# Ten more blocks turned by VectorE squares and memory, longer delays, branches mixer by mixer, in a decoder block on one core

## The chip, the cores and the metric

The kernel runs on one core of a Trainium2 chip. The metric is the device time of one execution in microseconds (us); of several executions the median is taken. Four engines share the work and run their own queues in order: TensorE (PE) multiplies and transposes, VectorE (DVE) and ScalarE (ACT) do the elementwise work, GpSimd (POOL) does a little of it and starts DMAs; SyncE (SP) only starts DMAs. An instruction waits at the head of its queue until its inputs are there and its output buffer is free, and all behind it on that engine wait with it.

## The reference

256 tokens of width 2048, float32, one layer. The functions of the parts are cut, and the lines of merged and of x are written shorter than they are.

```python
u = rms_norm(x, attn_norm[l])
proj = jnp.einsum('bsd,de->bse', u, w_in[l])
(fq, fk, fv, ff, cq, ckv, kpe, gqkv, gz, gb, ga, gate) = jnp.split(proj, split_idx, axis=-1)
o_fox = fox_mixer(fq, fk, fv, ff, fox_fgate_bias[l])
o_mla = mla_mixer(cq, ckv, kpe, mla_q_norm[l], mla_kv_norm[l], w_mla_uq[l], w_mla_ukv[l], cos, sin)
o_gdn = gdn_mixer(gqkv, gz, gb, ga, gdn_conv[l], gdn_a_log[l], gdn_dt_bias[l], gdn_out_norm[l])
gates = jax.nn.sigmoid(gate).reshape(B, S, N_BRANCHES, D_MODEL)
merged = sum(gates[:, :, b] * jnp.einsum('bsc,cd->bsd', o_b, w_branch[l, b]) for b, o_b in enumerate((o_fox, o_mla, o_gdn)))
x = x + jnp.einsum('bsd,de->bse', merged, w_out[l])
h = rms_norm(x, mlp_norm[l])
x = x + jnp.einsum('bsf,fd->bsd', jnp.square(jax.nn.relu(jnp.einsum('bsd,df->bsf', h, w_up[l]))), w_down[l])
```

The three mixers have 8 heads of 128 each. Fox is causal softmax attention with a learned decay, MLA is causal attention on compressed queries and keys, and the gated delta rule (gdn) takes its q, k and v from gqkv, 3072 channels, through a causal convolution over 4 tokens and silu:

```python
def causal_depthwise_conv(x, w):
    K, C = w.shape
    return lax.conv_general_dilated(x, w[:, None, :], window_strides=(1,), padding=[(K - 1, 0)],
                                    dimension_numbers=('NWC', 'WIO', 'NWC'), feature_group_count=C)
```

It then solves, in chunks of 64 tokens, a unit triangular system whose entries are damped by the decays between two tokens.

## The kernel before

**Gemms.** Every product with a large weight goes through `gemm`. A chunk of weights is two tiles of 128 rows by 512 columns: SP loads it as `raw`, ACT rounds it to `wh` (L258), DVE subtracts to get the rest `wl` (L259), and PE runs twelve matmuls of 512 columns: for two tiles of rows and two halves of the tokens, wh times the rounded activations (L265), wl times them (L266) and wh times their rest (L267). `raw` has four buffers, `wh` and `wl` three each. After each chunk `tick` counts down what `later` has put off, and runs what is due. After the last chunk of a block of 512 columns `evac` reads the two sums out of PSUM.

**Order.** A side generator is stepped once a chunk by `weave`, its instructions placed behind the casts of the last chunk (`behind`, through `anchor`). What a step issues, and after how many chunks, is thus written in the kernel; the order of each engine's queue is fixed when the program is built.

**Stages**, in microseconds of the profile's span: latents 0 to 84; MLA's projections to 125; Fox columns with MLA's attention beside them to 261; the output gate z with Fox's attention to 320; gqkv, six blocks, to 476; the branch gates, twelve blocks, to 768, with the delta rule (`gdn`) beside them until some 696; the three branch products (w_branch) to 902; w_out to 991; w_up and w_down to the end.

**Two ways to turn a block** (256 tokens by 512 channels into channels by tokens). `fox_evac` for the four blocks of q and k, and `gqkv_evac` for six, let PE do it: eight transposes of 128x128 into PSUM (L626 `ft`, L703 `cv`), from which ACT and DVE read: Fox's copies into `fqT` and `fkT` (L629 and below), or the convolution, an ACT scaling (L705) and three DVE steps (L707) for each of four groups of channels. `turned`, for the branch sums (`acc`), w_out's and w_up's results, uses no PE: DVE transposes squares of 32x32 (L1067) into the first half of a tile `zy`, POOL's queue writes that to memory (L1069, `turn<-zy`, 512 KB) and reads it back reordered with four DMAs (L1072, `zy<-turn`, 128 KB each), and consumers run TURN = 8 chunks later, counted by `tick`: for the branches `halves_of` makes `mH` (ACT, L1081) and `mL` (DVE, L1082).

**The delta rule's side work.** `gdn` spreads the decays: `gcT` (L772) goes to memory and comes back to all partitions as `E` (L777); after nine steps DVE subtracts (L783). Later a substitution of 31 steps runs on DVE (`fs` L859, `NT` L861), its result goes through memory (`td`, then `DT`, L875), and after eight steps DVE squares it into `D` (L884), which the 32-wide matmuls `pO` and `pD` (`blocks_of`, L892) read.

**Branches.** The loop goes over the four blocks n of columns, and within it over mixers 2, 0, 1; the sum of a block is complete, and turned, after its third mixer. `reload` brings Fox's and MLA's outputs back from memory (`of`, `om`). w_out's gemm takes the first 12 of 16 rows of tiles of two blocks before their last four (LATE).

**Start.** `x_prep` transposes x beside the first gemm and squares it on ACT for the norm (L195).

## Time and profile before

| | |
|---|---|
| median of 3 executions | 1689.87 us (1687.35 to 1692.42) |
| profiled execution | 1695.37 us |
| span of its trace | 1693.4 us |
| mean granted PE clock | 0.996 |
| POOL busy | 113.9 us, 7% |
| weight loads from memory (SP's queue) | 311.07 MB of 356.55 MB moved |

The profile is of one execution. L numbers are lines of the kernel before; busy shares are of the span, and an engine is idle where it waits. A row of PE's timeline has start, duration, line, operation and, in brackets, the idle time ahead of it with what ended it.

### The profile page before, as it was taken

Reading aid. Unit: us, or ns where it says so; the run is one execution under the profiler, and the core shown is the slowest. Engines: PE = TensorE matmul, PEld = TensorE weight load, DVE = VectorE, ACT = ScalarE, POOL = GpSimd, SP = SyncE. Lnnn points to the kernel's source line nnn. Section 1 sums busy time; section 2 is a strip of 40 time slices with the busy share of each in tenths; the row PEclk is TensorE's granted clock in tenths of the full one; section 3 lists DMA queues with packets and bytes.
Section 4 is the critical chain, followed back from the end, with each engine's and each line's share of the span. In section 5 each row is a group of like instructions: output and inputs, shape, how many; then the busy total and the mean of one; then the engine's idle time right before and its main releaser. Section 6 shows DMA issues by size and latency. Waiting matters only on the chain.

```text
span 1693.4 us, 21572 instructions
## 1 busy us (share of the span) xinstructions
PE 1672.5 (99%) x8035; PEld 1404.3 (83%) x8035; DVE 1029.7 (61%) x1423; ACT 811.2 (48%) x1035; POOL 113.9 (7%) x202
## 2 busy tenths in 40 slices
PE   9999999999999999999999999999999999999997
PEld 8998889978788788888878888888888888888886
DVE  5755447677668745746666666555655566546655
ACT  5555446555645433544444555433544344434543
POOL 0000000000010100001210101100110011001100
PEclk9999999999999999999999999999999999999999
DMA  7765554766667654877888887856886688668863
GB/s 237 203 173 181 158 170 133 228 187 186 172 175 212 201 162 138 279 217 240 272 271 275 261 229 246 242 191 196 240 257 203 194 243 237 199 193 235 239 207 138
DMA packets 191626, 356.55 MB, mean 211 GB/s; under 512 B 18040, under 2 KB 40224, under 8 KB 191008
## 3 DMA queue, kind: packets, MB, share of 16 engines
q1 hardware_dynamic: 177616, 311.07, 60.6%
q0 software_dynamic: 13296, 43.29, 8.6%
q8 instruction: 63, 1.03, 0.3%
q10 hardware_dynamic: 608, 0.79, 0.1%
q14 instruction: 43, 0.35, 0.1%
HBM read 331.50 MB, written 23.61 MB: 210 GB/s over the span
## 4 chain that ended last, share of the span: by engine, by line
PE 86%; DMA 5%; DVE 4%; issue 3%; POOL 1%; ACT 1%; SPq 0%; DVEq 0%; POOLq 0%; ACTq 0%
PE mm L266 25%; PE mm L267 25%; PE mm L265 25%; DVE wl L259 2%; DMA zy<-turn 1%; DMA raw<-in_w_out_dram 1%; DMA raw<-in_w_in_dram 1%; DVE fs L859 1%; ACT wh L258 1%; DVE NT L861 0%; PE bf L508 0%; PE bf L509 0%; PE bf L510 0%; PE mm L1202 0%; PE mm L1201 0%
## 5 line engine op out<-in xcount | busy, mean ns | idle before, releaser
L259 DVE TENSOR_TENSOR wl<-raw,wh 128x1024 fp32r<-128x1024 f32 (+3 forms) x552 | 663.0, 1203 | 523.1 <-ACT wh L258 520.6
L258 ACT CAST wh<-raw 128x1024 fp32r<-128x1024 f32 (+3 forms) x552 | 571.5, 1037 | 688.2 <-PE mm L267 635.1
L266 PE MATMUL mm<-wl,uH 128*128 128x512 f32 (+3 forms) x896 | 346.0, 386 | 2.8 <-DVE wl L259 2.8
L267 PE MATMUL mm<-wh,uL 128*128 128x512 f32 (+3 forms) x896 | 343.9, 384 | 0.0
L265 PE MATMUL mm<-wh,uH 128*128 128x512 f32 (+3 forms) x896 | 319.6, 386 | 1.3 <-ACT wh L258 1.3
L266 PE MATMUL mm<-wl,hH 128*128 128x512 f32 x512 | 199.2, 389 | 0.0
L267 PE MATMUL mm<-wh,hL 128*128 128x512 f32 x512 | 199.2, 389 | 0.0
L266 PEld LDWEIGHTS mm<-wl,uH 128*128 128x128 f32 x896 | 169.4, 189 | 35.6 <-DVE wl L259 5.8
L265 PEld LDWEIGHTS mm<-wh,uH 128*128 128x128 f32 x896 | 168.1, 189 | 31.6 <-ACT wh L258 1.7
L267 PEld LDWEIGHTS mm<-wh,uL 128*128 128x128 f32 x896 | 169.2, 189 | 29.5
L266 PE MATMUL mm<-wl,dH 128*128 128x512 f32 x480 | 186.9, 389 | 0.1
L267 PE MATMUL mm<-wh,dL 128*128 128x512 f32 x480 | 186.8, 389 | 0.0
L265 PE MATMUL mm<-wh,hH 128*128 128x512 f32 x512 | 178.4, 389 | 0.0
L265 PE MATMUL mm<-wh,dH 128*128 128x512 f32 x480 | 167.2, 389 | 0.0
L266 PEld LDWEIGHTS mm<-wl,hH 128*128 128x128 f32 x512 | 96.1, 188 | 20.0
L267 PEld LDWEIGHTS mm<-wh,hL 128*128 128x128 f32 x512 | 96.1, 188 | 20.0
L265 PEld LDWEIGHTS mm<-wh,hH 128*128 128x128 f32 x512 | 96.1, 188 | 19.9
L266 PEld LDWEIGHTS mm<-wl,dH 128*128 128x128 f32 x480 | 90.1, 188 | 19.3 <-DVE wl L259 0.5
L267 PEld LDWEIGHTS mm<-wh,dL 128*128 128x128 f32 x480 | 90.1, 188 | 18.6
L265 PEld LDWEIGHTS mm<-wh,dH 128*128 128x128 f32 x480 | 90.0, 188 | 18.6
L1072 POOL DMA_DIRECT2D zy<-turn x96 | 52.4, 553 | 101.5 <-ACT wh L258 32.8
L1069 POOL DMA_DIRECT2D turn<-zy x24 | 13.3, 556 | 646.1 <-DVE zy L1067 646.1
(425 smaller groups left out, 1776.5 us busy)
## 6 DMA issues: line engine op xcount, KB each, us to landing
raw<-in_w_in_dram SPq DMA_DIRECT2D x192, 512.0 KB, 3.9
raw<-in_w_up_dram SPq DMA_DIRECT2D x128, 512.0 KB, 4.3
raw<-in_w_down_dram SPq DMA_DIRECT2D x128, 512.0 KB, 4.6
raw<-in_w_branch_dram SPq DMA_DIRECT2D x48, 512.0 KB, 5.1
raw<-in_w_out_dram SPq DMA_DIRECT2D x32, 512.0 KB, 4.9
turn<-zy POOLq DMA_DIRECT2D x24, 512.0 KB, 3.3
zy<-turn POOLq DMA_DIRECT2D x96, 128.0 KB, 5.6
gd<-ge POOLq DMA_DIRECT2D x24, 256.0 KB, 4.8
```

The costliest lines, as they stand in the source:

```text
L258: h = A.copy(out=wh[:, :, :n], in_=raw[:, :, :n])
L259: l = V.tensor_tensor(out=wl[:, :, :n], in0=raw[:, :, :n], in1=wh[:, :, :n].bitcast(F32), op=ALU.subtract)
L265: PE.matmul(ps[t][:, :n], lhsT=lhsH(k, t), rhs=wh[:, kk, :n], start=(k == 0), stop=False)
L266: PE.matmul(ps[t][:, :n], lhsT=lhsH(k, t), rhs=wl[:, kk, :n], start=False, stop=False)
L267: PE.matmul(ps[t][:, :n], lhsT=lhsL(k, t), rhs=wh[:, kk, :n], start=False, stop=last)
L859: V.tensor_tensor(out=tmp[:, :, 0:i + 1], in0=T[:, :, 0:i + 1], in1=Nb[:, 0:i + 1, i].unsqueeze(1).broadcast_to([P, 16, i + 1]), op=ALU.mult)
L1069: nc.gpsimd.dma_start(out=d, in_=z)
L1072: nc.gpsimd.dma_start(out=y[32 * j:32 * j + 32].rearrange("a (g x) -> a g x", g=4), in_=dv[j])
```

## The change

`turned` stands further up and serves ten more blocks: the four of Fox's queries and keys (TURN, now 10 chunks of delay) and the six of gqkv (13 chunks). `fox_heads` (an ACT copy for each half of the tokens) and `by_channel` (two copies into `ch`), then `conv` in two parts, read from SBUF a turned block. The 80 PE transposes of those blocks are gone. The branches wait 9 chunks, w_out's blocks 8, w_up's 10. E is subtracted after 14 steps, D after 12, the substitution has more steps towards its end, and what needs the convolution waits for it (`convolved`). The branch loop has the mixers outside (0, 1, 2) and the columns inside, with all four sums in one long tile; the reloads start 80 steps into the gates beside the delta rule. w_out takes 8 rows of tiles ahead where it took 12. The squares of x are put behind the last casts of the first gemm.

```diff
-TURN = 8
-LATE = 12
+TURN = 10
...
         for t in range(2):
-            for q in range(4):
-                j = t2("junk")
-                A.activation(out=j, in_=xs[t][:, q * 512:(q + 1) * 512], func=AF.Square, accum_out=ssx[:, t, q:q + 1])
+            with behind():
+                for q in range(4):
+                    j = t2("junk")
+                    A.activation(out=j, in_=xs[t][:, q * 512:(q + 1) * 512], func=AF.Square, accum_out=ssx[:, t, q:q + 1])
...
-        e = me("fe")
+        e = fe[t] = me("fe")
         scaled_evac(e, ps, t)
-        pt = psx("ft").rearrange("p (a t) -> p a t", a=4)
-        for a in range(4):
-            PE.transpose(pt[:, a, :], e[:, a * P:(a + 1) * P], ident)
+        if t == 1:
+            turned([fe[0], fe[1]], *[lambda y, t=t: fox_heads(bi, y, t) for t in range(2)])
+
+    def fox_heads(bi, y, t):
+
         h0 = (bi % 2) * 4
-        if bi < 2:
-            A.activation(out=fqT[:, h0:h0 + 4, t * P:(t + 1) * P], in_=pt, func=AF.Copy, scale=-(HD ** -0.5))
-        else:
-            ev_copy(fkT[:, h0:h0 + 4, t * P:(t + 1) * P], pt)
+        d = (fqT if bi < 2 else fkT)[:, h0:h0 + 4, t * P:(t + 1) * P].rearrange("p k (g b) -> p k g b", b=32)
+        yt = y.rearrange("p (g t k b) -> p t k g b", g=4, t=2, k=4)[:, t]
+        A.activation(out=d, in_=yt, func=AF.Copy, scale=-(HD ** -0.5) if bi < 2 else 1.0)
...
+        turned([gx[0], gx[1]], lambda y: by_channel(y, bi), lambda y: conv(y, bi, 0), lambda y: conv(y, bi, 1), delay=13)
+
+    chans, convolved = {}, set()
+
+    def by_channel(y, bi):
+
+        u = chans[bi] = big("ch")[:, 0:1024].rearrange("p (k t) -> p k t", k=4)
+        yv = y.rearrange("p (g t k b) -> p t k g b", g=4, t=2, k=4)
+        for t in range(2):
+            ev_copy(u[:, :, t * P:(t + 1) * P].rearrange("p k (g b) -> p k g b", b=32), yv[:, t])
+
+    def conv(_, bi, a):
+        u = chans[bi]
+        y = t2("y").rearrange("p (a b) -> p a b", a=2)
+        for b in range(2):
+            c = 2 * a + b
+            ct = bi * 4 + c
+            A.activation(out=y[:, b, :], in_=u[:, c, :], func=AF.Copy, scale=cw[:, 72 + ct:73 + ct])
...
-        for _ in wait(9):
+        for _ in wait(14):
             yield
...
+            while not {(g, 1), (g + 2, 1)} <= convolved:
+                yield
...
             if i % 2 or i > 12:
                 yield
+            if i > 20:
+                yield
...
-        for _ in wait(8):
+        for _ in wait(12):
             yield
...
-    weave(gates(0, 12), chain(delta, *again))
-    run(delta)
+    mixers = both(delta, chain(idle(80), *again))
+    weave(gates(0, 12), mixers)
+    run(again[0])
...
-    for n in range(4):
-        acc = [t2("acc") for _ in range(2)]
-        for i, b in enumerate((2, 0, 1)):
+    acc = [big("acc") for _ in range(2)]
+    for b in range(3):
+        if b == 1:
+            run(again[1])
+        if b == 2:
+            run(mixers)
+        for n in range(4):
...
-    weave(gemm(by_tile(mH), by_tile(mL), w_out[0], 0, 16, [(n * 512, 512) for n in range(4)], out_evac, True), load_x2())
+    weave(gemm(by_tile(mH), by_tile(mL), w_out[0], 0, 16, [(n * 512, 512) for n in range(4)], out_evac, 8), load_x2())
```

Three places in the engines' queues. First DVE where the decays go out and come back as E, in gqkv's stage (`gcT` to memory, `E` from it, `y<-cv` the convolution, `wl` the weights' rest, one to a chunk; `zy<-gq` squares of a turned block). Before:

```order
L772 COPY gcT_3222<-pr_686_3220 16x128
L707 SCALAR_TENSOR_TENSOR y_706_3323<-cv_705_3322,cw_117,y_706_3323 128x255
L707 SCALAR_TENSOR_TENSOR y_708_3338<-cv_707_3337,cw_117,y_708_3338 128x255
L707 SCALAR_TENSOR_TENSOR y_706_3323<-cv_705_3322,cw_117,y_706_3323 128x254
L707 SCALAR_TENSOR_TENSOR y_708_3338<-cv_707_3337,cw_117,y_708_3338 128x254
L707 SCALAR_TENSOR_TENSOR y_706_3323<-cv_705_3322,cw_117,y_706_3323 128x253
L259 TENSOR_TENSOR wl_725_3429<-raw_723_3426,wh_724_3428 128x1024
L707 SCALAR_TENSOR_TENSOR y_708_3338<-cv_707_3337,cw_117,y_708_3338 128x253
L259 TENSOR_TENSOR wl_728_3453<-raw_726_3450,wh_727_3452 128x1024
L259 TENSOR_TENSOR wl_731_3477<-raw_729_3474,wh_730_3476 128x1024
L707 SCALAR_TENSOR_TENSOR y_706_3323<-cv_705_3322,cw_117,y_706_3323 128x255
L783 TENSOR_SCALAR E_687_3226<-E_687_3226,gc_682_3200 128x128 x12
```

and now:

```order
L803 COPY gcT_3218<-pr_686_3216 16x128
L259 TENSOR_TENSOR wl_723_3404<-raw_721_3401,wh_722_3403 128x1024
L360 STREAM_TRANSPOSE zy_705_3318<-gq_703_3314 128x4x4x32
L360 STREAM_TRANSPOSE zy_705_3318<-gq_704_3316 128x4x4x32
L259 TENSOR_TENSOR wl_726_3422<-raw_724_3419,wh_725_3421 128x1024
L259 TENSOR_TENSOR wl_729_3440<-raw_727_3437,wh_728_3439 128x1024
L259 TENSOR_TENSOR wl_732_3458<-raw_730_3455,wh_731_3457 128x1024
L259 TENSOR_TENSOR wl_741_3491<-raw_739_3488,wh_740_3490 128x1024
L259 TENSOR_TENSOR wl_744_3509<-raw_742_3506,wh_743_3508 128x1024
L814 TENSOR_SCALAR E_687_3222<-E_687_3222,gc_682_3196 128x128 x4
```

Between gcT and the first subtraction of E (L783, now L814) there were three wl, and there are six; the convolution's steps are gone from there, and two squares of the first gqkv block stand in it.

Second DVE where the substitution ends (`fs`, `NT`) and its result comes back through memory as DT, to be squared into D. Before:

```order
L861 TENSOR_REDUCE NT_939_4512<-fs_952_4591 128x16
L859 TENSOR_TENSOR fs_952_4591<-NT_939_4512 128x512
L259 TENSOR_TENSOR wl_1065_5259<-raw_1063_5256,wh_1064_5258 128x1024
L861 TENSOR_REDUCE NT_939_4512<-fs_952_4591 128x16
L259 TENSOR_TENSOR wl_1068_5277<-raw_1066_5274,wh_1067_5276 128x1024
L259 TENSOR_TENSOR wl_1075_5303<-raw_1073_5300,wh_1074_5302 128x1024
L259 TENSOR_TENSOR wl_1078_5321<-raw_1076_5318,wh_1077_5320 128x1024
L884 STREAM_TRANSPOSE D_1079_5336<-DT_1042_5136 32x16x32 x2
```

and now, the last rows ahead of D:

```order
L259 TENSOR_TENSOR wl_1158_5741<-raw_1156_5738,wh_1157_5740 128x1024
L259 TENSOR_TENSOR wl_1165_5767<-raw_1163_5764,wh_1164_5766 128x1024
L259 TENSOR_TENSOR wl_1168_5785<-raw_1166_5782,wh_1167_5784 128x1024
L259 TENSOR_TENSOR wl_1171_5803<-raw_1169_5800,wh_1170_5802 128x1024
L259 TENSOR_TENSOR wl_1174_5821<-raw_1172_5818,wh_1173_5820 128x1024
L259 TENSOR_TENSOR wl_1177_5839<-raw_1175_5836,wh_1176_5838 128x1024
L919 STREAM_TRANSPOSE D_1178_5854<-DT_1127_5576 32x16x32 x3
```

Three wl lay between the last NT and D; now the last NT (an L894) stands eleven rows above the first row of this piece, with ten wl in between, and sixteen wl lie between it and D.

Third ACT at the end of the first gemm (`wh` its weight casts, L282, `uH` the rounded x, `junk<-x` the squares of x). Before, further up:

```order
L152 ACTIVATE uH_5_110<-tr_39_213,gcol_92 128x256
L282 CAST wh_44_242<-raw_43_240 128x736
L195 ACTIVATE junk_84_494,ssx_10_114<-x0_1_85 128x512
L195 ACTIVATE junk_85_496,ssx_10_114<-x1_2_86 128x512
L195 ACTIVATE junk_86_498,ssx_10_114<-x1_2_86 128x512
L195 ACTIVATE junk_87_500,ssx_10_114<-x1_2_86 128x512
L195 ACTIVATE junk_88_502,ssx_10_114<-x1_2_86 128x512
L152 ACTIVATE uH_5_110<-tr_46_260,gcol_92 128x256
```

and now:

```order
L282 CAST wh_79_471<-raw_78_469 128x736
L195 ACTIVATE junk_81_488,ssx_10_114<-x0_1_85 128x512
L195 ACTIVATE junk_82_490,ssx_10_114<-x0_1_85 128x512
L195 ACTIVATE junk_83_492,ssx_10_114<-x0_1_85 128x512
L195 ACTIVATE junk_84_494,ssx_10_114<-x0_1_85 128x512
L195 ACTIVATE junk_85_496,ssx_10_114<-x1_2_86 128x512
L195 ACTIVATE junk_86_498,ssx_10_114<-x1_2_86 128x512
L195 ACTIVATE junk_87_500,ssx_10_114<-x1_2_86 128x512
L195 ACTIVATE junk_88_502,ssx_10_114<-x1_2_86 128x512
L282 CAST wh_101_528<-raw_100_526 128x736
```

The squares stood in two groups near the fifth cast; now all eight stand in one row between the last two casts of the first gemm.

## The prediction

> **What bounds the kernel now.** I read the page's busy shares first, then TensorE's waits, then the groups of ACT and the chain that ended last.

> ```profile
> span 1693.4 us, 21572 instructions
> ...
> PE 1672.5 (99%) x8035; PEld 1404.3 (83%) x8035; DVE 1029.7 (61%) x1423; ACT 811.2 (48%) x1035; POOL 113.9 (7%) x202
> ```

> TensorE is busy 99% of the span; DVE at 61% and ACT at 48% feed it. So there are two ways to a shorter time: less work on PE, or fewer of the places where PE stands. The list of PE's waits shows how little the second can give (total us, times, longest):

> ```profile
> PE mm L266 <- DVE wl L259: 3.9, 6, 1.8
> PE pO L892 <- DVE D L884: 2.3, 1, 2.3
> PE mm L265 <- ACT wh L258: 1.5, 2, 1.3
> ...
> PE bf L508 <- ACT fqT L629: 0.7, 1, 0.7
> ```

> That is 8.4 us of 1693. ACT, on the other side, runs ahead of PE, and the group of the weight casts says by what it is held:

> ```profile
> L258 ACT CAST wh<-raw 128x1024 fp32r<-128x1024 f32 (+3 forms) x552 | 571.5, 1037 | 688.2 <-PE mm L267 635.1
> ```

> ```profile
> ACT mH L1081: 14.2, 3
> ```

> It idles 688 us, 635 of it until PE gives a wh buffer back. The second row is from the view of tile zy, its list of who waited for it (us, times): three times ACT stood at an mH copy, 14.2 us in all, 4.7 us each, and PE lost some 0.5 us each time (below). So an instruction of ACT that is late by up to about 4.2 us costs PE nothing. This allowance is what I weigh every new wait against.

> **Eighty transposes leave PE.** PE's timeline (start, duration):

> ```profile
> 152.82 0.39 PE L266 MATMUL mm<-wl,uH 128*128 128x512 f32 x1
> ...
> 155.54 0.39 PE L266 MATMUL mm<-wl,uH 128*128 128x512 f32 x1
> 155.78 1.03 PE L626 MATMUL ft<-cst,fe 128*128 128x128 f32 x8
> 156.65 0.39 PE L600 MATMUL lg<-knT,qnT 128*128 128x128 f32 x2
> ```

> From 152.82 to 155.54 run twelve gemm matmuls, one chunk: 2.72 us, 0.227 each. Eight transposes take the stretch from 155.78 to 156.65: 0.87 us, 0.109 each, although one alone is shown as 0.27 long (they overlap). The groups give the counts:

> ```profile
> L703 PE MATMUL cv<-cst,gq 128*128 128x128 f32 x48 | 9.0, 273 | 0.0
> ...
> L626 PE MATMUL ft<-cst,fe 128*128 128x128 f32 x32 | 4.1, 272 | 0.0
> ```

> 48 + 32 = 80, and none had to wait. They stand on the engine that bounds, so 80 x 0.109 = **8.7 us** goes. The 16 transposes of the values (L720) stay.

> **The wait for E goes.** On the chain that ended last, and on PE just behind:

> ```profile
> 345.53 4.21 DMA gcd<-gcT
> ...
> 350.38 7.10 DMA E<-gcd
> ```

> ```profile
> 364.49 0.39 PE L267 MATMUL mm<-wh,uL 128*128 128x512 f32 x1
> 366.68 0.50 PE L266 MATMUL mm<-wl,uH 128*128 128x512 f32 x1 [1.80 <-DVE wl L259]
> ```

> E lands at 357.48, 12.0 us after the start of gcd's write; DVE stands before E's subtraction (L783), the wl behind it are late, then the wh, and PE waits twice. What a wait costs is the pitch less 0.227: 366.68 - 364.49 - 0.227 = 1.96, 0.16 more than the 1.80 marked; with as much on the other, the 1.3 of wh in PE's list, 1.44: **3.4 us**. In the new order six wl subtractions lie between gcT and the first E row, 6 x 2.72 = 16.3 us. Late next is nothing that I find: 4 us remain, and then the allowance.

> **The wait for the diagonal blocks goes.** Chain, then PE:

> ```profile
> 577.98 4.35 DMA td<-NT
> ...
> 585.74 3.94 DMA DT<-td
> ```

> ```profile
> 589.93 0.34 PE L892 MATMUL pO<-D,E 32*32 32x32 f32 x6 [2.30 <-DVE D L884]
> ...
> 591.72 0.79 PE L266 MATMUL mm<-wl,uH 128*128 128x512 f32 x1 [0.42 <-DVE wl L259]
> ...
> 595.23 0.40 PE L266 MATMUL mm<-wl,uH 128*128 128x512 f32 x1
> ```

> PE loses 2.30, then 0.42, and then runs from 591.72 to 595.23 at half pace: nine pitches in 3.51 us, of which nine at 0.227 would be 2.04, so 1.5 more. Two windows of the profile, with the granted clock third from the end (0.16 of 10 us, and 0.11 of 15 us, are lost in them, 1.6 us each):

> ```profile
> 585.00:595.00 10.00, 7.28 (x36) 5.34 (x35) 5.69 (x6) 2.04 (x2) 3.53 (x7) 0.84 0.51 152
> 600.00:615.00 15.00, 15.00 (x148) 12.47 (x145) 5.53 (x6) 4.62 (x6) 0.00 (x0) 0.89 0.46 135
> ```

> Sum **4.2 us**. From td's start to DT landed it takes 585.74 + 3.94 - 577.98 = 11.7 us; in the new order sixteen wl lie between the last row of the substitution and D, 43 us. Late next: nothing.

> [...]

> **Smaller waits.** Of the rows on wl and wh above there remain 3.9 - 1.80 - 0.42 and 1.5 - 1.28, together 1.9 us in five places: one in the substitution (DVE full of fs beside the convolution, which in the new order ends ahead of it) and four at the turned branch blocks. For those the chain has

> ```profile
> 803.99 5.31 DMA turn<-zy
> ...
> 811.25 7.60 DMA zy<-turn
> ```

> The turn's write starts at 803.99 and its rows are back at 818.85; with two DVE squares of 0.69 ahead of it (row below) a turn takes 16.5 us. The order before gives it 5 chunks, 13.6 us; the new one 8, 6, 6 and 8 chunks, 16.3 to 21.8 us. So 1.9 us go, and the 0.7 us of the last row on PE's waits too, since fqT no longer stands ahead of mla_proj: **2.6 us**.

> **What is added.** Prices from the groups of DVE and ACT:

> ```profile
> L707 DVE SCALAR_TENSOR_TENSOR y<-cv,cw,y 128x255 f32<-128x255 f32 (+2 forms) x72 | 31.8, 476 | 2.7 <-ACT y L705 2.3
> ...
> L1067 DVE STREAM_TRANSPOSE zy<-r 128x512 f32<-128x512 f32 x32 | 20.8, 686 | 0.0
> ...
> L195 ACT ACTIVATE junk<-x 128x512 f32<-128x512 f32 x8 | 5.0, 633 | 1.6 <-DMA x<-in_x_dram 1.6
> ```

> from the windows (length, then busy time of PE, PEld, DVE, ACT, POOL), and from tile zy on POOL's issues (ns, least, median, most):

> ```profile
> 365.00:476.00 111.00, 109.32 (x499) 88.56 (x500) 77.22 (x120) 67.07 (x89) 0.00 (x0) 1.00 0.63 181
> 476.00:590.00 114.00, 111.11 (x500) 90.62 (x499) 89.22 (x141) 56.00 (x62) 19.17 (x27) 1.00 0.68 196
> ```

> ```profile
> L1072 POOL DMA_DIRECT2D zy<-turn x96: 550/552/576, 809.6 to 1604.7; - x96
> ```

> - Ten turned blocks: 20 squares on DVE x 0.686 = 13.7 us, 50 DMAs on POOL x 0.55 = 27.5 us, and 12 copies into ch on ACT and DVE at 0.6 to 0.7 (nearest: the square of as many elements, 0.633 on ACT, and the DVE square, 0.686). DVE has 34 us and 25 us free in the two windows, and POOL is 7% busy over the span: hidden behind PE. The convolution's 72 steps read SBUF where they read PSUM; no row has the same shape from SBUF, so I leave 0.476 and bound the change at 0.1 us each way, 7 us of DVE, under the same cover.
> - The tightest of the ten is the first gqkv block: in the new order 8 chunks lie between its squares and its first reader, 21.8 us, against 16.5 us measured plus up to 2 us in which its write stands on POOL behind E's. Left: 3 us, then the allowance. If the cover were gone, each late microsecond would cost one.
> - All eight squares of x stand in one row on ACT, between two weight casts: from the group, 8 x 0.62 = 5.0 us with their reads. ACT's casts are two chunks of some 2 us ahead there, so about 4.2 us is hidden: 0.8 us (0 to 1.5).
> - In gqkv's stage the first ch copies stand ahead of a wh and wait for the turn: 0 to 1.5, I take 0.5. Bursts of 5 to 6 us on DVE and ACT where the convolution of one block meets E, and in the gates' stage: two, 0 to 1.5 each; I take 0.5 each.
> - Branches mixer by mixer: the same 48 chunks and 24 gate reads; acc in one long tile, the same shapes. The reloads move to 80 chunks into the gates, and POOL's gate reads stand behind no turn before the last mixer. Zero, hidden behind PE.

> **Sum.** 8.7 + 3.4 + 4.2 + 2.6 = 18.9 us gone; 0.8 + 0.5 + 1.0 = 2.3 us new. Net 16.6. The profiled execution took 1695.4 us, 2.0 more than its span; it becomes 1678.8. That execution lies 5.5 us above the median of the runs, 1689.87; the same 16.6 us off the median gives 1673.3, **1673 us**.

> **Rivals.**
> 1. *Only the transposes are gained.* The waits of 8.4 us and their aftermath come back at other instructions: PE's queue is in order, and a wait moved to another place is still one. For it: 50 more DMAs and longer delays that rest on a landing time seen once each. Against: the order leaves 4, 31 and 3 us. It gives 1689.9 - 8.7 + 2.3 = 1683.5 at worst, 1680 to 1684 in all.
> 2. *DVE becomes the bound* between 340 and 590. For it: 78% busy in 476 to 590, and 13.7 us of squares plus some 4 us of copies added where E, convolution and substitution already are. Against: the convolution is moved out of the substitution's window. If all 17.7 us reached PE: 1673 + 14 to 18, 1687 to 1691, no change to speak of.
> 3. *The round trip is longer than the delay, slower than before.* Place: ACT's reader of each turned block, with wh queued behind it and PE behind wh. To eat the 16.6 us and 5 more, ten blocks must lose 2.2 us each, so a trip of 21.8 + 4.2 + 2.2 = 28 us, against the 16.5 measured; at 29 us it is 1705. For it: POOL issues in order, and E's, gd's and nd's DMAs share its queue. Against: the longest landings of the chain above.
> 4. *The clock.* The second of the two windows above has its half pace behind the 32-wide matmuls of pD (L892), which stay; if it goes as well, another 1.6 us goes, 1671.5; if the first stays, 1674.5.

> [...]

> **How the numbers follow.** Forecast (1668 to 1678) 0.63; rival 4 0.09; rival 1 0.17; rival 2 0.06; rival 3 0.05. The range takes the forecast, the clock and rival 1 except its end: 1665 to 1683. A measurement of this kernel tells about 0.3% (5 us) from no change; so faster is 0.63 + 0.09 + 0.17 = 0.89, same 0.06, slower 0.05.

> **What would show it.** Right: no L626 and L703 on PE, PE's waits for wl and wh under 2 us, none for D, PE busy about 15 us less. The turned blocks: no wait of ACT for zy over 4 us between 130 and 480. Wrong: rows of PE waiting for wh behind fqT, fkT or ch (rival 3), for wl with DVE over 90% in a window (rival 2), or a new stretch at a granted clock under 0.9.

## The result and the profile after

The changed kernel took 1671.71 us (median of four executions, 1670.66 to 1672.68), the kernel before 1690.48 in the same comparison: a ratio of 0.9891, 95% interval 0.9873 to 0.9908, or 18.4 us less (15.6 to 21.5). A second session gave 0.9886 (0.9864 to 0.9907). The profiled execution is the one of 1670.66 us.

The page of the changed kernel has (span, busy times, then the chain that ended last by engine):

```profile
span 1668.9 us, 21530 instructions
...
PE 1656.0 (99%) x7955; PEld 1395.1 (84%) x7955; DVE 1038.9 (62%) x1447; ACT 810.1 (49%) x1039; POOL 141.2 (8%) x252
...
PE 98%; DMA 0%; ACT 0%; SPq 0%; DVE 0%; issue 0%; DVEq 0%
```

The span is 24.5 us shorter, more than the 18.4 of the runs: the execution of before that was profiled lay 4.9 us above the median, that of the changed kernel 1.0 below. PE is busy 16.5 us less; DVE has 9.2 us more, POOL 27.3, as 50 more DMA issues at 0.55 us make it. The whole list of PE's waits is now

```profile
PE mm L289 <- ACT wh L282: 2.0, 2, 1.5
PE warm L125 <- DVE ones L107: 1.1, 1, 1.1
PE mm L289 <- ACT uH L151: 0.7, 1, 0.7
```

All three are in the first 45 us. In this profile not one wait for E, D, wl in the substitution, or the branches is left, and the chain that ended last, in which PE had 86% before, DMA 5%, DVE 4% and issue 3%, is PE nearly to the start.

How close it was shows on POOL and ACT at the first gqkv block (start, duration, line, idle time ahead):

```profile
341.41 0.52 POOL L805 DMA_DIRECT2D gcd<-gcT  x1 [47.65 <-DVE gcT L803]
345.31 0.57 POOL L808 DMA_DIRECT2D E<-gcd  x1 [3.37 <-DMA gcd<-gcT]
345.87 0.55 POOL L362 DMA_DIRECT2D turn<-zy  x1
356.01 2.21 POOL L365 DMA_DIRECT2D zy<-turn  x4 [9.60 <-DMA turn<-zy]
```

```profile
364.66 0.61 ACT L347 COPY ch<-zy 128x512 f32<-128x512 f32 x1
```

The block's squares began at 343.73 on DVE. Its write is issued right behind E's, lands 9.9 us later, at about 355.8, and the reader runs at 364.66 without having waited. The trace has the last of the four reads landing at 364.37, so the trip took 20.6 us and 0.3 us were left. In the second profile it took 21.7, and ACT stood for it, at no cost to PE:

```profile
365.35 0.63 ACT L347 COPY ch<-zy 128x512 f32<-128x512 f32 x1 [0.57 <-DMA zy<-turn]
```

Two prices that no row of before had, from the groups of DVE:

```profile
L737 DVE SCALAR_TENSOR_TENSOR y<-ch,cw,y 128x255 f32<-128x255 f32 (+2 forms) x72 | 30.6, 476 | 0.1
...
L349 DVE COPY ch<-zy 128x512 f32<-128x512 f32 x6 | 2.6, 440 | 0.0
```

The convolution's step costs the same 476 ns from SBUF as it did from PSUM, and the copy into ch 0.44 us on DVE.

### The profile page after: what moved, and what is told of

Same layout as the page of the kernel before. It is cut to its first block, busy times and chain, and to the rows that moved or that the text cites. A ratio compares the mean times of both kernels' runs of the same rounds, so it can differ in the third digit from the quotient of the medians.

```text
span 1668.9 us, 21530 instructions
## 1 busy us (share of the span) xinstructions
PE 1656.0 (99%) x7955; PEld 1395.1 (84%) x7955; DVE 1038.9 (62%) x1447; ACT 810.1 (49%) x1039; POOL 141.2 (8%) x252
## 3 DMA queue, kind: packets, MB, share of 16 engines
q0 software_dynamic: 16656, 53.78, 10.8%
## 4 chain that ended last, share of the span: by engine, by line
PE 98%; DMA 0%; ACT 0%; SPq 0%; DVE 0%; issue 0%; DVEq 0%
PE mm L265 30%; PE mm L266 30%; PE mm L267 30%; PE bf L528 0%; PE bf L529 0%; PE bf L527 0%; PE mm L1236 0%; PE mm L1234 0%; PE mm L1235 0%; PE pg L867 0%; PE po L443 0%; DMA raw<-in_w_in_dram 0%; PE bt L514 0%; PE bt L516 0%; PE bt L515 0%; PE pT L436 0%
## 5 line engine op out<-in xcount | busy, mean ns | idle before, releaser
L259 DVE TENSOR_TENSOR wl<-raw,wh 128x1024 fp32r<-128x1024 f32 (+3 forms) x552 | 663.4, 1202 | 525.0 <-ACT wh L258 521.9
L258 ACT CAST wh<-raw 128x1024 fp32r<-128x1024 f32 (+3 forms) x552 | 572.3, 1037 | 716.9 <-PE mm L267 672.5
L266 PE MATMUL mm<-wl,uH 128*128 128x512 f32 (+3 forms) x896 | 342.6, 382 | 0.0
L267 PE MATMUL mm<-wh,uL 128*128 128x512 f32 (+3 forms) x896 | 341.1, 381 | 0.0
L265 PE MATMUL mm<-wh,uH 128*128 128x512 f32 (+3 forms) x896 | 317.1, 385 | 0.0
L266 PE MATMUL mm<-wl,hH 128*128 128x512 f32 x512 | 199.2, 389 | 0.0
L267 PE MATMUL mm<-wh,hL 128*128 128x512 f32 x512 | 199.2, 389 | 0.0
L266 PEld LDWEIGHTS mm<-wl,uH 128*128 128x128 f32 x896 | 168.4, 188 | 30.1 <-DVE wl L259 0.3
L267 PEld LDWEIGHTS mm<-wh,uL 128*128 128x128 f32 x896 | 168.3, 188 | 30.0
L265 PEld LDWEIGHTS mm<-wh,uH 128*128 128x128 f32 x896 | 167.6, 188 | 30.4
L267 PE MATMUL mm<-wh,dL 128*128 128x512 f32 x480 | 186.7, 389 | 0.0
L266 PE MATMUL mm<-wl,dH 128*128 128x512 f32 x480 | 186.7, 389 | 0.0
L265 PE MATMUL mm<-wh,hH 128*128 128x512 f32 x512 | 178.4, 389 | 0.0
L265 PE MATMUL mm<-wh,dH 128*128 128x512 f32 x480 | 167.3, 389 | 0.0
L266 PEld LDWEIGHTS mm<-wl,hH 128*128 128x128 f32 x512 | 96.1, 188 | 19.9
L267 PEld LDWEIGHTS mm<-wh,hL 128*128 128x128 f32 x512 | 96.1, 188 | 20.0
L265 PEld LDWEIGHTS mm<-wh,hH 128*128 128x128 f32 x512 | 96.1, 188 | 20.0
L266 PEld LDWEIGHTS mm<-wl,dH 128*128 128x128 f32 x480 | 90.1, 188 | 18.7
L267 PEld LDWEIGHTS mm<-wh,dL 128*128 128x128 f32 x480 | 90.1, 188 | 18.6
L265 PEld LDWEIGHTS mm<-wh,dH 128*128 128x128 f32 x480 | 90.0, 188 | 18.7
L365 POOL DMA_DIRECT2D zy<-turn x136 | 74.3, 553 | 144.4 <-DMA turn<-zy 51.6
L362 POOL DMA_DIRECT2D turn<-zy x34 | 19.0, 558 | 763.4 <-DVE zy L360 668.1
```

The costliest lines, as they stand in the source:

```text
L258: h = A.copy(out=wh[:, :, :n], in_=raw[:, :, :n])
L259: l = V.tensor_tensor(out=wl[:, :, :n], in0=raw[:, :, :n], in1=wh[:, :, :n].bitcast(F32), op=ALU.subtract)
L265: PE.matmul(ps[t][:, :n], lhsT=lhsH(k, t), rhs=wh[:, kk, :n], start=(k == 0), stop=False)
L266: PE.matmul(ps[t][:, :n], lhsT=lhsH(k, t), rhs=wl[:, kk, :n], start=False, stop=False)
L267: PE.matmul(ps[t][:, :n], lhsT=lhsL(k, t), rhs=wh[:, kk, :n], start=False, stop=last)
L362: nc.gpsimd.dma_start(out=d, in_=z)
```

## The experiments

Ratios are to the kernel before in the same session; 0.001 is 1.7 us. None of these kernels leaves out work of the reference; pe_extra adds work whose result nothing reads.

| kernel | ratio | 95% interval |
|---|---|---|
| changed | 0.9891, again 0.9886 | 0.9873 to 0.9908, 0.9864 to 0.9907 |
| pe_turn: PE turns the ten blocks again | 0.9954 | 0.9939 to 0.9969 |
| waits_only: only the longer waits | 0.9956 | 0.9938 to 0.9974 |
| turn_only: the ten turned blocks, the waits as before | 0.9896 | 0.9881 to 0.9911 |
| turn_e14: these and E's wait | 0.9881 | 0.9865 to 0.9897 |
| pe_extra: 80 transposes added that nothing reads | 0.9934 | 0.9920 to 0.9948 |
| e9: E after 9 steps | 0.9897 | 0.9874 to 0.9919 |
| d0: no steps ahead of D | 0.9879 | 0.9857 to 0.9901 |
| delay4: gqkv's readers after 4 chunks | 0.9950 | 0.9934 to 0.9966 |
| branch_old: branches as before | 0.9892 | 0.9877 to 0.9907 |
| sqspread: squares of x spread | 0.9869, again 0.9885 | 0.9847 to 0.9891, 0.9870 to 0.9901 |

**Which part carries the gain.** Four kernels.

pe_turn is the changed kernel with `fox_evac` and `gqkv_evac` as before, of which the core:

```diff
-            turned([fe[0], fe[1]], *[lambda y, t=t: fox_heads(bi, y, t) for t in range(2)])
...
+        for a in range(4):
+            PE.transpose(pt[:, a, :], e[:, a * P:(a + 1) * P], ident)
```

waits_only is the kernel before with

```diff
-        for _ in wait(9):
+        for _ in wait(14):
...
+            if i > 20:
+                yield
...
-        for _ in wait(8):
+        for _ in wait(12):
```

turn_only is the changed kernel with these three undone, and the branches and the squares of x too; turn_e14 is turn_only with E's wait at 14 again. Both still have, besides the ten blocks, the reloads' new start, the long tile for the sums and w_up's 10 chunks.

> The changed kernel with the ten blocks turned by PE again (80 transposes), all delays, the branch order and the squares as changed. Theory (the terms add up: transposes on PE, and waits that the longer delays remove by themselves): 7.6 to 8.7 us over the changed kernel's 1671.7, 1679.5 to 1680.5, and no wait of PE for E or D, since in its order six chunks lie ahead of E and sixteen ahead of D. Rival (the waits went because the convolution no longer stands on DVE beside E and the substitution): PE waits for wl come back around E and in the substitution, 1684 or more.

> The kernel before with only three numbers changed: E after 14 steps, D after 12, more steps late in the substitution; PE turns all ten blocks. Theory: E's 3.4 and D's 4.2 to 6 us go, 1681 to 1683. Rival (a wait that is moved comes back elsewhere): 1688 to 1691.

> The kernel before with only the ten blocks turned through memory: E after 9 steps, D after 8, no more steps in the substitution, columns outside in the branches, squares without an anchor. Theory: 7.6 for the transposes, 0.8 for fqT no longer ahead of mla_proj, 0.7 for the substitution beside the convolution, off 1690.5, 1681.4; and as its order has eleven chunks between the substitution and D also the 4.2 to 6 us at D, so 1676 to 1677; E's 3.4 us and the branches' 1.5 stay. Rival (only transposes): 1682 to 1683, with D's wait in it.

> The kernel before with two of the changes: the ten blocks turned through memory, and E after 14 steps. The branches, D's 8 steps, the substitution's steps and the squares as before. Theory (these two carry nearly all; the third place, D, is cleared by the convolution's leaving DVE): what is left is 0 to 1.5 us at the branches, so 0 to 1 us above the changed kernel. Rival (the longer waits at D and the branch order have a part of their own): 4 us or more above.

pe_turn was 0.0063 slower than the changed kernel, 10.7 us: more than its theory's 7.6 to 8.7, less than its rival's 12 and more. Its trace has neither E's nor D's wait, as the theory said; what came back is the wait in mla_proj, 0.7, and two for wl in the substitution, 0.8 (two more, 1.3, stand in w_out, where a second profile of the changed kernel has them too). waits_only gained 7.4 us, at the small end of its theory (1681 to 1683 from 1690.5): the waits for E and D went, and nothing of their size came back (one wait of 0.5 for wl at 1259 us is new). turn_only gained 17.6 us, more than its theory's 13.5 to 14.5; the theory kept 1.5 us of waits at the branches, of which this trace has none, and took 7.6 us for the transposes, which is too little (below). Of PE's waits behind the start only those of E are left in it:

```profile
PE mm L264 <- ACT wh L257: 1.9, 1, 1.9
...
PE mm L265 <- DVE wl L258: 0.4, 1, 0.4
```

(lines are one lower there). With E's 14 steps too, turn_e14, the ratio is 0.9881, beside 0.9886 for the changed kernel in that session: two of the edits do all that can be measured, though PE still waits 1.4 us at the branches in its trace. The parts overlap, since D's wait goes with either end (7.4 + 17.6 is 25.0, not 18.4). Why it goes with the turned blocks alone, though D has its 8 steps as before, shows in the built order; counted in wl on DVE's queue, the last NT of the substitution and the first D stand at

```
               last NT   first D
before             197       200
waits_only         199       215
turn_only          201       212
d0                 201       204
changed            211       227
```

The steps ahead of D are counted by the program, while before the substitution ran beside the convolution on a full DVE (busy 46.07 of the 47 us from 530 to 577). I take the three chunks in place of eleven as the backlog of that; it is read from the orders, and no run of its own was made for it.

**The price of the transposes.** pe_extra has the 80 transposes of before again, into PSUM that nothing reads.

```diff
         e = fe[t] = me("fe")
         scaled_evac(e, ps, t)
+        pt = psx("ft").rearrange("p (a t) -> p a t", a=4)
+        for a in range(4):
+            PE.transpose(pt[:, a, :], e[:, a * P:(a + 1) * P], ident)
```

(and likewise eight to a block in gqkv_evac.)

> The changed kernel with the 80 transposes of before added again on PE, into PSUM tiles that nothing reads; everything else as changed. It measures the price of the transposes by themselves. Theory: 7.7 us for the transposes in their own rows and 0.09 us longer for the gemm matmul that follows each of some 20 to 26 groups, so 9.6 to 10 us above the changed kernel, a ratio of 0.9945 against 0.9888, with no new wait of PE. Rival (0.109 us each and nothing around them): 8.7. Second rival (of the 10.7 us by which the kernel with PE's turns was slower, waits around the convolution were more than 3): 7 or less.

0.9934 against 0.9891 and 0.9886: 7.3 to 8.1 us, where each of the three ratios is known to 2.4 to 3.6 us either way. From the start of each transpose to the start of what follows it on PE, its trace has 3.3 us for the 32 and 4.3 for the 48, 7.6 together, and a gemm matmul behind a group of them is 0.09 us longer, 1.0 us for the eleven groups (of 16) that have one behind them: 8.6. The theory's 9.6 to 10 took 20 to 26 such groups. In the kernel before the transposes stood more scattered, and its trace counted the same way has 7.0 us (without PE's wait for fqT, 0.66) and 2.0 for 23 of 27 groups, 9.0. So the transposes are some 8 to 9 us of the gain. pe_turn's trace has 7.1 + 1.9 for them, and 1.8 for the wait at fqT and the two in the substitution (0.66, and 0.24 + 0.55 with 0.16 more each): 10.8, beside the 10.7 measured. The intervals alone would not part 10.7 from 8.

**E and D.**

```diff
 # e9
-        for _ in wait(14):
+        for _ in wait(9):
 # d0
-            if i > 20:
-                yield
-        for _ in wait(12):
+        for _ in wait(0):
```

> The changed kernel with E after 9 steps, as before. In its order E's first subtraction stands three chunks behind gcT, 8.2 us, where E landed 12 to 13 us behind. Theory: DVE stands some 4.6 us, wl behind it, PE loses 2 to 3.5 us: 1674 to 1675. Rival (without the convolution's steps DVE has room and the buffers cover it): 1671.7, no wait of PE for wl there.

> The changed kernel with no wait steps ahead of D and without the added steps of the substitution; its order has three chunks between the substitution and D, 8.2 us, where the way through memory takes 11.7 to 13. [...] Rival: the allowance covers it, 1671.7.

DVE stood 5.66 us in e9 and 5.60 in d0, and 7.16 at D in the kernel before. DVE's rows in e9, d0 and the kernel before, one each:

```profile
355.04 2.44 DVE L814 TENSOR_SCALAR E<-E,gc 128x128 f32<-128x128 f32 x12 [5.66 <-DMA E<-gcd]
```

```profile
582.88 0.70 DVE L917 STREAM_TRANSPOSE D<-DT 32x512 f32<-32x512 f32 x1 [5.60 <-DMA DT<-td]
```

```profile
588.97 1.43 DVE L884 STREAM_TRANSPOSE D<-DT 32x512 f32<-32x512 f32 x2 [7.16 <-DMA DT<-td]
```

PE's list of e9 has 2.7 us in one wait, and it is for wh: ACT stood too, at its own next step on E, with the cast behind it.

```profile
PE mm L265 <- ACT wh L258: 2.7, 1, 2.7
```

```profile
355.95 0.63 ACT L815 ACTIVATE E<-E 128x512 f32<-128x512 f32 x1 [5.11 <-DVE E L814]
...
357.27 1.03 ACT L258 CAST wh<-raw 128x1024 fp32r<-128x1024 f32 x1
```

In d0 nothing of ACT's waits for D, and one square of 0.70 us stands between D's landing and the next wl, where e9 has twelve subtractions, 2.44 us. PE's list of d0 has

```profile
PE mm L266 <- DVE wl L259: 0.9, 2, 0.5
...
PE pO L925 <- DVE D L917: 0.3, 1, 0.3
```

Of these, 0.3 for D and 0.5 for the wl behind it are this place, 0.8 where I had expected 2 to 3 (1674 to 1675). The runs tell neither kernel from the changed one. So e9's profile bears the theory out in size, though the wait came through wh and not wl, and in d0 the rival was nearer: the same 5.6 us on DVE cost 0.8 or 2.7, by what stands behind it on DVE and on ACT; which of the two weighs more, no run parts. In e9's profiled execution, the slowest of its four, the clock also fell to 0.50 for 3.4 us behind that wait (359.7 to 363.1), 1.7 us more.

**The readers of gqkv's blocks.**

```diff
-lambda y: conv(y, bi, 0), lambda y: conv(y, bi, 1), delay=13)
+lambda y: conv(y, bi, 0), lambda y: conv(y, bi, 1), delay=4)
```

> The changed kernel with the readers of gqkv's turned blocks put off by 4 chunks in place of 13. Its order still has 6, 5, 5, 4, 11 and 4 chunks between the squares and their readers (10.9 to 16.3 us), against trips of 21 us for the first block and 14 for the others. Theory (an ACT instruction may be late by some 4.2 us at no cost): 0.5 us for the first block, nothing for the others, up to 2 in all: 1672 to 1674. Rival (each late microsecond reaches PE): 4.7 + 0 + 0.4 + 3.1 + 0 + 3.1, 1683.

The theory fell: 0.9950, 10 us slower than the changed kernel, 1682 if set on the first session's 1690.5, beside the rival's 1683. ACT's rows of delay4 show the mechanism that my prediction had as its slower rival:

```profile
364.93 0.62 ACT L347 COPY ch<-zy 128x512 f32<-128x512 f32 x1 [4.71 <-DMA zy<-turn]
365.46 1.04 ACT L258 CAST wh<-raw 128x1024 fp32r<-128x1024 f32 x1
366.40 1.71 ACT L735 ACTIVATE y<-ch,cw 128x256 f32<-128x256 f32 x4
...
397.00 0.62 ACT L347 COPY ch<-zy 128x512 f32<-128x512 f32 x1 [5.92 <-DMA zy<-turn]
...
422.29 0.62 ACT L347 COPY ch<-zy 128x512 f32<-128x512 f32 x1 [6.64 <-DMA zy<-turn]
```

and PE's list

```profile
PE mm L266 <- DVE wl L259: 5.6, 7, 1.5
PE mm L265 <- ACT wh L258: 2.5, 3, 1.2
```

In time PE loses 4.7 us in four stalls behind the first copy, 2.3 in three behind the second and 2.0 in two behind the third, and one stretch at half clock follows at 426 us (3.4 us, 1.7 lost): 10.7 together. Beyond the allowance of 4.2 ACT stood 0.5, 1.7 and 2.4 us, so for the second and third block the allowance comes near; there the theory went wrong on the trips, which took 16.3 and 15.5 us, not 14. At the first block PE lost 4 us more than the excess: behind the copy stand the convolution and, among its steps, E's subtractions, and DVE's wl come 4.5 and 4.1 us apart where PE uses one in 2.72.

```profile
366.69 1.22 DVE L259 TENSOR_TENSOR wl<-raw,wh 128x1024 fp32r<-128x1024 f32 x1
...
371.19 1.22 DVE L259 TENSOR_TENSOR wl<-raw,wh 128x1024 fp32r<-128x1024 f32 x1
...
375.28 1.22 DVE L259 TENSOR_TENSOR wl<-raw,wh 128x1024 fp32r<-128x1024 f32 x1
```

The rival's sum came out by luck: it had 4.7, 0, 0.4, 3.1, 0 and 3.1 reach PE, and PE lost its time at the first three blocks alone. Taking nine steps of delay away costs more than half of what the change gains.

**The branches.**

```diff
-    for b in range(3):
-        if b == 1:
-            run(again[1])
-        if b == 2:
-            run(mixers)
-        for n in range(4):
+    run(again[1])
+    run(mixers)
+    for n in range(4):
+        for i, b in enumerate((2, 0, 1)):
...
-                    turned([acc[tt][:, n * 512:(n + 1) * 512] for tt in range(2)], *[lambda y, t=t: halves_of(y, n, mHt, mLt, t) for t in range(2)], delay=9)
+                    turned([acc[tt][:, n * 512:(n + 1) * 512] for tt in range(2)], *[lambda y, t=t: halves_of(y, n, mHt, mLt, t) for t in range(2)], delay=8)
...
-    weave(gemm(by_tile(mH), by_tile(mL), w_out[0], 0, 16, [(n * 512, 512) for n in range(4)], out_evac, 8), load_x2())
+    weave(gemm(by_tile(mH), by_tile(mL), w_out[0], 0, 16, [(n * 512, 512) for n in range(4)], out_evac, 12), load_x2())
```

> The changed kernel with the columns outside and the mixers (2, 0, 1) inside in the branches, 8 chunks of delay there, w_out taking 12 row tiles ahead. Theory: the three waits behind mH come back, 1.5 us: 1673.2, PE's waits 1.5 us longer and ACT waiting some 14 us for zy at mH. Rival (they were an effect of where the delta rule's end or the reloads fell): 1671.7 and no wait at mH.

0.9892 to 0.9891: nothing that can be measured. The trace agrees with the theory in kind: ACT waited 15.9 us in three places at mH, 6.2 the longest, and PE lost 2.3 us there. But turn_only has the same branches, and ACT waited 10.3 us there, 4.2 the longest, and PE not at all. The trip through memory differs from execution to execution (20.6 and 21.7 us for the first gqkv block in the two profiles of the changed kernel), and the old order stands on that edge; and the new one has some of it too, since in the second profile of the changed kernel ACT waited 6.7 us at mH, 4.2 the longest, and PE 1.0 us in w_out.

**The squares of x.**

```diff
+    def square(i):
+        t, q = i % 2, i // 2
+        j = t2("junk")
+        A.activation(out=j, in_=xs[t][:, q * 512:(q + 1) * 512], func=AF.Square, accum_out=ssx[:, t, q:q + 1])
...
             yield
             if q:
+                with behind():
+                    square(q - 1)
                 yield
+        with behind():
+            square(7)
         nc.sync.dma_start(out=cst[:, P:], in_=consts[:, P:])
-        for t in range(2):
-            with behind():
-                for q in range(4):
-                    j = t2("junk")
-                    A.activation(out=j, in_=xs[t][:, q * 512:(q + 1) * 512], func=AF.Square, accum_out=ssx[:, t, q:q + 1])
```

> The changed kernel with one square of x behind the casts of each second chunk of the first gemm in place of eight in a row. Theory: the 0.57 us in which PE waited for wh at 43 us goes, 1671.1 (0.4 to 1.0 less); and if ACT's work near the start delays a cast there, nothing is gained. Rival (the raw loads set the start, not ACT): 1671.7.

> The changed kernel itself, in one session with the next two, so that they can be set against it: 0.989 of the kernel before.

> The changed kernel with one square of x behind the casts of each second chunk of the first gemm, once more, beside the changed kernel. Theory: 0.6 us less than that, a ratio lower by 0.0003, which is less than a measurement tells; its profile has no wait of PE at 43 us. Rival (the first session's ratio, 0.9869 against 0.9891, is real and comes from elsewhere): 3 us or more less.

The first session looked like 3.7 us; side by side the two are at 0.9885 and 0.9886. The wait at 43 us is gone from the traces of sqspread, as the theory said, and 0.6 us can't be told in the time. No kernel of this study is measurably faster than the changed one; turn_e14, d0 and sqspread stand level with it.

## Why the prediction was right

The forecast was 1673 us and 16.6 us of gain, the measured time 1671.7 and 18.4. Point by point:

- **Transposes, 8.7.** Right in kind, and in size by some luck: 7.3 to 8.1 by pe_extra, 9.0 by the rows of before. The pitch of 0.109 came from a run of eight; in the convolution's pairs a transpose takes 0.07 until the next starts. On the other side the 0.09 us behind each group was left out.
- **E, 3.4.** The wait is gone; put back by e9, PE loses 2.9, and in the profiled execution a stretch of half clock behind it. The margin I named, 4 us, was there: E landed at 353.8, and the first subtraction ran at 358.5.
- **D, 2.7 of stall.** Gone, but not by the edit I gave it to. The prediction had sixteen wl ahead of D from the longer wait; turn_only clears D with the 8 steps of before, and d0 with none loses 0.8. The edit would have done it alone, too (waits_only).
- **The clock, 1.5.** This term was too small, and no run shows it by itself: the stretch at half pace stands in the profile of before, but that it goes with D's stall was my estimate, from its place right behind it. The runs have in its place the mean of the whole: 35 executions of the kernel before in these sessions have a mean granted clock of 0.9963, eight of the changed one 0.9981: 0.0018 of 1690, 3.0 us; the five of waits_only, whose profile has no wait for D, have 0.998 to 0.999. I counted the stretch at half pace behind D, and left that behind pD as a rival, which the first profile bears out and the second does not (last section).
- **Smaller waits, 2.6.** Those of mla_proj and the substitution went. At the branches it was less sure than I had it: in the traces the old order costs 0 to 2.3 us, the new one 0 to 1.6 (pe_turn).
- **What is added, 2.3.** Squares 0.8: 0.57 measured. ch 0.5 and the bursts 1.0: no wait found. DVE in the window from 476 to 590 was busy 88.1 us, against 89.2 before.
- **The margin of the first gqkv block.** I put the trip at 18.5 us and the margin at 3; it took 20.6 with 0.3 left, and 21.7 in the second profile, where nothing was left and the allowance took the 0.57 us. E's DMA did not only go first; the write ran beside it, and took 9.9 us where the median of before is 3.3. The conclusion held, but not on the margin that I gave for it.

Set together from runs and traces: 8 to 9, 3, 2.7, 3.0 and 2, less 0.6, is 18 to 19, beside the 18.4 of the runs. The terms are not independent (the parts measured one by one add up to 25.0), so this doesn't prove each of them. The forecast had the clock too small by 1.5 and the added work too large by 1.7, and on the other side 1.0 too much for E and the smaller waits; in part these errors cancel, which is luck. Of the rivals, the first (waits that come back) and the second (DVE) did not come. The third, the slower one, did not come either, but delay4 shows that its threshold was set wrong: I took late microseconds as free up to 4.2 and then one for one, and asked for a trip of 28 us; with trips of 21 us and less, and readers two to seven chunks earlier, it already costs 10. (By its own sum a trip of 29 us gives 1703, not 1705.)

## What to carry to other kernels

Work that leaves the bound engine brings its own price (here 8 to 9 us of 18.4); the waits that go with it can bring as much again, so count what else stood on the helper engines beside it (here the convolution on DVE beside the substitution). In these runs a late instruction on a helper engine was free only up to the lead of that engine, and less where more work stood right behind it or a second helper waited for the same thing: ACT's 4.2 us at mH in turn_only cost PE nothing, its 4.71 at the first ch copy in delay4 cost 4.7, DVE's 5.60 at D in d0 cost 0.8 and its 5.66 at E in e9, where ACT stood too, 2.7. Where data goes through memory, give its reader the longest trip measured beside the other DMAs of that stage, not the median of a quiet one.

## What the runs showed of the hardware

Half clock came without PE being idle. In the second profile of the changed kernel PE runs 32-wide matmuls up to the gemm, and then the gemm at a pitch of 0.427 us, where a chunk of before has 0.227 (PE's timeline, then two windows with the granted clock third from the end):

```profile
660.13 1.99 PE L927 MATMUL pD<-DT,OD 32*32 32x32 f32 x61
...
663.15 0.63 PE L265 MATMUL mm<-wh,uH 128*128 128x512 f32 x1
663.58 0.63 PE L266 MATMUL mm<-wl,uH 128*128 128x512 f32 x1
```

```profile
655.00:662.00 7.00, 7.00 (x115) 6.02 (x113) 3.41 (x4) 3.92 (x5) 1.08 (x2) 1.00 0.67 205
662.00:666.00 4.00, 4.00 (x14) 3.16 (x12) 0.22 (x1) 0.58 (x1) 0.00 (x0) 0.57 0.60 177
```

PE is shown busy 7.00 of 7.00 us ahead of it. The granted clock fell 655.4 us after it had risen at the start, and for 3.4 us. In the profile of before it is at 0.50 twice, for 3.413 us each, behind the stall for D and behind pD's matmuls:

```profile
588.32:591.73 3.41, 1.38 (x17) 0.89 (x17) 2.67 (x4) 0.39 (x1) 1.12 (x2) 1.00 0.35 134
591.73:595.14 3.41, 3.41 (x8) 2.73 (x9) 3.02 (x3) 0.00 (x0) 0.00 (x0) 0.50 0.75 195
605.38:608.80 3.42, 3.42 (x100) 3.03 (x98) 1.91 (x3) 1.62 (x2) 0.00 (x0) 1.00 0.59 159
608.80:612.21 3.41, 3.41 (x10) 2.73 (x9) 0.16 (x1) 0.58 (x1) 0.00 (x0) 0.50 0.55 156
```
